# One scaling per attention step, value sums on GpSimd, and a new table of output products

## The chip, the cores and the metric

The kernel runs on one core of a Trainium2 chip. The metric is the device time of one launch in microseconds (us); lower is better. The kernel before took 1141.24 us in the median of three runs (1140.78 to 1141.5).

A core has five engines with one instruction queue each: TensorE (PE in the profile; PEld is its weight load), VectorE (DVE), ScalarE (ACT), GpSimd (POOL) and SyncE (SP), which here only issues transfers. An engine takes its instructions in order. It waits at an instruction for semaphores that other engines raise, and everything behind that instruction waits too. Matmuls write to PSUM, of which the kernel allots eight tiles of 128x512 f32; the rest of the data lies in SBUF.

## The reference

A decoder of two layers over 512 tokens of width 1024, all in f32: layer 0 mixes positions in chunks with a gated MLP; then one shared set of keys and values is computed; layer 1 is sliding-window attention over them. Each layer also has a gated MLP and a gated embedding. The change lies in layer 1's attention:

```
q = (xn @ w_q).reshape(B, nb, BLOCK, N_KV_HEADS, GQA_GROUP, HEAD_DIM)
scores = einsum('bnikgd,bnjkd->bnkgij', q, kblk) * HEAD_DIM ** -0.5
scores = where(valid, scores - slopes * dist, -inf)       # a band of 128 keys
m = maximum(max(scores, -1), sink)
e = exp(scores - m)
probs = e / (sum(e, -1) + exp(sink - m))
out = einsum('bnkgij,bnjkd->bnikgd', probs, vblk)
h = h + out.reshape(B, S, N_Q_HEADS * HEAD_DIM) @ w_o
```

There are 16 query heads of 64 channels in 4 groups (a group shares a key and value head), and 4 blocks of 128 tokens.

## The kernel before

**Numbers as pairs.** TensorE multiplies in a reduced f32 format, so every operand is split in a high part (a copy in that format) and a low part (the rest). A product is three matmuls: high by high, high by low, low by high (`mm3`, lines 181 to 183 of its inner loop). "Products" below counts matmuls of 128x128 by 128x512. Weights come in pieces of 1 MB by SyncE's transfers into `wraw`; `pump` splits each in two units, on ScalarE (`wh`, line 154) and VectorE (`wl`, line 155).

**Attention in steps.** A step is one group of heads and one block of tokens: 16 steps, `steps[i]`. The loop runs i from 0 to 17 and handles three steps at once:

- `scores(i)`: eight score matmuls into two PSUM tiles (`sc`, lines 781 and 782). VectorE picks the keys of the band from the own and the previous block (`copy_predicated`, line 784) and adds the slope with a reduction to the row's extremum (line 788). ScalarE takes four exponentials with their sums (line 793). GpSimd puts the sinks in place (line 774). The result lies in one of two halves of `prs`.
- `weights(i)`: reciprocals of the sums (line 801), then each of the four heads' weights times its reciprocal, one on VectorE (line 807) and three on ScalarE (line 805).
- `turn(i - 1)`: four transposes to PSUM (`tr`, line 822), split in `pts` (ScalarE line 252, VectorE line 253); for blocks after the first, GpSimd also cuts the part for the previous block out of both (line 830).
- `mix(i - 2)`: two or four matmuls with the values (`pv`, line 844). One half of the result's partitions holds the products with the high part of the values, the other those with the low part. They are summed: ScalarE copies the one half to `side` (line 848) and VectorE adds the other from PSUM (line 852, two instructions). Then ScalarE makes `oh` (line 856) and GpSimd `ol` (line 857), the pair that the output projection takes.

`side` is double-buffered by the parity of the step, and its copy's half was always the same partitions.

**Work beside the steps.** TensorE would stand still while the other engines do this, so the table `beside` names projection products to be issued with each step: first the values and the queries of the next groups (`project`), then the output projection (`merge(m, k0, k1)`: accumulator `o{m}`, contraction blocks k0 to k1, three matmuls each). `merge` opens its accumulator's PSUM tile at k0 = 0 and keeps it until it is complete. In steps 10 to 17 the table has 9, 9, 9, 9, 12, 6, 18 and 18 products. `more` splits one more unit of weights ahead of its use. What remains of the output projection follows the loop, where each accumulator is added to `h`.

**The order.** The order of instructions on each engine isn't written out: a scheduler takes it from the program's order, from its own idea of durations, and from priorities (`scores`, `turn` and `weights` are high). So an edit of one helper can move instructions of others. In the changed program's order of TensorE, the first pv matmul of step k is followed by transposes of step k + 1 mixed with scores of step k + 3, then the rest of pv, then the products. An exception is step 12: its first pv matmul stands right behind the last of step 11.

**Transfers of queries.** Groups 1 to 3 need their queries on other partitions, so four transfers per half group on SyncE's queue move them (lines 661 and 662), beside the loads of weights.

Of the kernel before, what the change touches and what calls it, by code (L numbers as in the profile page):

```python
# [8 lines left out]
F32 = mybir.dt.float32  # L9
F32R = mybir.dt.float32r  # L10
AF = mybir.ActivationFunctionType
ALU = mybir.AluOpType

P = 128
D = 1024
S = 512
# [10 lines left out]
GQ = HEADS // GROUPS  # L27
# [21 lines left out]
def tile_yoco(ctx: ExitStack, tc: tile.TileContext, t, out: bass.AP, out_b: bass.AP):  # L49
    nc = tc.nc  # L50
# [10 lines left out]
    def psum(name):  # L61
        return mmp.tile([P, S], F32, tag="mm", name=name)


    pieces, paired = [], set()

    def plan(ap_, n, cols, own=None):

        if own and len(own) > 1:
            m = n // len(own)  # L70
            cuts = [(q * m, m) for q in range(len(own))]
        else:
            m = n if n <= UNIT else (n // cols + 1) // 2 * cols
            cuts = [(0, m), (m, n - m)] if m < n else [(0, n)]
        pieces.append((ap_, n, cuts, own))

    def plan_cols(w, n_chunks, kk, cols=256, k0=0):
        for c in range(n_chunks):
            plan(w[c, :, k0 * cols : (k0 + kk) * cols], kk * cols, cols)
# [6 lines left out]
    def plan_ffn(l):  # L86
        for i, (j0, j1) in enumerate(PARTS):
            if i == 0:
                plan_cols(t["w_up"][l], j1, KD)
            else:  # L90
                plan_cols(t["w_up"][l, j0 + 1 : j1], j1 - j0 - 1, KD)
            if i + 1 < len(PARTS):
                plan_cols(t["w_up"][l, j1 : j1 + 1], 1, KD)
            else:
                plan(t["pT"][l], 2 * S, S, own=[(mp, "m4", "m5")])
                plan_cols(t["w_pin"][l], 2, 4)
            plan_cols(t["w_down"][l], 4, j1 - j0, k0=j0)
# [9 lines left out]
    plan_cols(t["w_q"][0:1], 1, KD)  # L107
    plan_cols(t["w_kv"][1:2], 1, KD)
    plan_cols(t["w_q"][1:4], 3, KD)
    plan_cols(t["w_o"], 4, KD)  # L110
    plan_ffn(1)
    free = [j % SLOTS for j in range(NJ, NJ + 8)]
# [4 lines left out]

    units = [(i, q, lo, n) for i, p in enumerate(pieces) for q, (lo, n) in enumerate(p[2])]
    raws, ready = {}, {}
    state = {"raw": 0, "unit": 0, "next": 0, "tags": [0, 1, 2], "turn": 0, "pt": 0}  # L120

    def load(upto, queue=nc.sync):
        while state["raw"] < min(upto, len(pieces)):
            j = state["raw"]
            a, m = pieces[j][:2]
            tags = state["tags"]
            r = wp.tile([P, 2 * UNIT], F32, tag=f"r{tags[state['turn'] % len(tags)]}", bufs=1, name=f"wraw{j}")
            state["turn"] += 1
            queue.dma_start(r[:, :m].rearrange("p (c m) -> p c m", c=2) if j in paired else r[:, :m], a)
            raws[j] = r  # L130
            state["raw"] += 1

# [70 lines left out]
    h = [hp.tile([P, S], F32, tag=f"h{k}", name=f"h{k}") for k in range(KD)]  # L203
    nc.sync.dma_start(vec[:, :KD], t["vec"][:, :KD])
    load(1, nc.scalar)
    for c in range(2):
        nc.sync.dma_start(h[0][:, c * N : (c + 1) * N], t["xT"][0][:, c * N : (c + 1) * N])
    load(2)
    nc.sync.dma_start(h[1], t["xT"][1])
    load(3)  # L210
# [18 lines left out]
    ps = psum("idle").rearrange("p (a b) -> p a b", a=4)  # L229
# [331 lines left out]
    for c in range(4):  # L561
# [4 lines left out]
        for j in range(2):  # L566
            m = 2 * c + j
            ps = ups[j]
# [13 lines left out]
            hi = ap.tile([P, S], F32R, tag=f"ah{m}", name=f"ush{m}")  # L582
# [10 lines left out]
    ps = psum("turned")  # L593
# [18 lines left out]
    sides = [slice(0, HD), slice(HD, P)]  # L612
# [28 lines left out]
    def queries(ps, g, j):  # L641


        qf = tp.tile([P, S], F32, tag="sq", name=f"qf{g}_{j}")
        m = 2 * g + j
        nc.vector.scalar_tensor_tensor(qf, ps, qscale[:, m : m + 1], rstd, op0=ALU.mult, op1=ALU.mult)
        res = [tp.tile([P, S], F32R, tag=("hs", "sg", "c0", "c1")[2 * j + e], name=f"q{g}_{j}_{e}")
               for e in range(2)]
        if g == 0:
            for e, q in enumerate(res):  # L650
                me, it = sides[e], sides[1 - e]
                nc.scalar.copy(q[me, :], qf[me, :])
                nc.vector.tensor_sub(q[it, :], qf[me, :], q[me, :].bitcast(F32))
            return res

        hi = tp.tile([P, S], F32, tag="acc", name=f"qhi{g}_{j}")
        nc.scalar.copy(hi.bitcast(F32R), qf)
        nc.vector.tensor_sub(qf.bitcast(F32R), qf, hi)
        for e, q in enumerate(res):
            me, it = sides[e], sides[1 - e]  # L660
            nc.sync.dma_start(q[me, :].bitcast(F32), hi[me, :])
            nc.sync.dma_start(q[it, :].bitcast(F32), qf[me, :])
        return res

    qs = {0: []}
    for j in range(2):
        qs[0] += queries(qps[j], 0, j)
# [42 lines left out]
    def project(g, j, k0, k1):  # L710
        if j == 0 and k0 == 0:
            box["q"] = chunk(256, KD, ahead=2)
            qs[g] = []
        if k0 == 0:
            box["qp"] = psum(f"q{g}_{j}")
        mm3(box["qp"], box["q"][k0:k1], xq[k0:k1], j * P, first=k0 == 0, last=k1 == KD)
        if k1 == KD:
            qs[g] += queries(box["qp"], g, j)
# [10 lines left out]
    def more():  # L729
# [12 lines left out]
        7: [(project, 3, 0, 4, 8), (more,)],  # L742
        8: [(project, 3, 1, 0, 4)],
        9: [(project, 3, 1, 4, 8)],
        10: [(merge, 0, 0, 3), (more,)],
        11: [(merge, 0, 3, 4), (merge, 1, 0, 2), (more,)],
        12: [(merge, 1, 2, 4), (merge, 2, 0, 1)],
        13: [(merge, 2, 1, 4)],
        14: [(merge, 0, 4, 6), (merge, 1, 4, 6)],
        15: [(merge, 2, 4, 6)],  # L750
        16: [(merge, 3, 0, 6)],
        17: [(merge, 4, 0, 6)],
    }

    def fill(i):
# [41 lines left out]
    def weights(i):  # L797

        pr, sm = live[i]
        ds = at.tile([P, GQ], F32, tag="ds", bufs=2, name=f"ds{i}")  # L800
        nc.vector.reciprocal(ds, sm)
        for e in range(GQ):
            a, r = pr[:, e, :P], ds[:, e : e + 1]
            if e:
                nc.scalar.activation(a, a, AF.Copy, scale=r)
            else:
                nc.vector.tensor_scalar_mul(a, a, r)
        live[i] = pr

    def pair(name):  # L810
# [24 lines left out]
    def mix(i):  # L835
        g, n = steps[i]
        pts = live.pop(i)
        ps = psum(f"pv{i}")
        todo = []
        for b, halves in enumerate(pts):  # L840
            both_halves = (diffs[g][:, n - 1] if b else vt[:, n, g]).rearrange("p a d -> p (a d)")
            todo += [(both_halves, x) for x in halves]
        for j, (lhs, rhs) in enumerate(todo):
            nc.tensor.matmul(ps, lhs, rhs, start=j == 0, stop=j == len(todo) - 1)


        low = side[sides[0], i % 2 * S : (i % 2 + 1) * S]
        nc.scalar.copy(low, ps[sides[1], :])
        o = side[:, 2 * S + i % 2 * N : 2 * S + (i % 2 + 1) * N].rearrange("p (b t) -> p b t", b=2)
        a, low = (x.rearrange("p (b e t) -> p e b t", b=2, e=2) for x in (ps[sides[0], :], low))  # L850
        for e in range(2):
            nc.vector.tensor_add(o[sides[e]], a[:, e], low[:, e])
        cols = slice(n * P, (n + 1) * P)
        for b in range(2):
            oh, ol = o2[2 * g + b]
            nc.scalar.copy(oh[:, cols], o[:, b, :])
            (nc.vector if i == last - 1 else nc.gpsimd).tensor_sub(ol[:, cols], o[:, b, :], oh[:, cols].bitcast(F32))

    last = len(steps)
    side = at.tile([P, 4 * S], F32, tag="vtl", name="side")  # L860
# [3 lines left out]
    for i in range(last + 2):  # L864
        if i < last:
            with tc.high_priority():
                scores(i)
        if i <= last:
            fill(i)
        if i >= 2:  # L870
            mix(i - 2)
        if i > last:
            fill(i)
        if 0 <= i - 1 < last:
            with tc.high_priority():
                turn(i - 1)
        if i < last:
            with tc.high_priority():
                weights(i)
# [46 lines left out]
    for i in range(2):  # L926
# [4 lines left out]
        for q in range(2):  # L931
            ps = psum(f"ht{i}_{q}")
# [4 lines left out]
    for m in range(4):  # L937
        ps = psum(f"gate{4 + m}")[:, :N]
# [32 lines left out]
    def gate_t(i, n):  # L971

        c0, w = cuts[i][n]
        ps = psum(f"gt{i}_{n}")[:, :w]
        end = i == 1 and n == len(cuts[i]) - 1
        if end:
            nc.tensor.matmul(ps, rows[:, :P], rows[:, P : 3 * P], start=True, stop=False)
        mm3t(ps, xs, parts2 if c0 >= S else parts, c0 % S, w, 2 + i, first=not end)
        return ps
# [57 lines left out]
    ps = gate_t(0, 1)  # L1037
# [72 lines left out]
```

## Time and profile before

| what | before |
|---|---|
| median of three runs | 1141.24 us |
| profiled execution, whole | 1141.22 us |
| its span on the core | 1139.5 us |
| TensorE busy | 1127.0 us (99%) |
| VectorE busy | 749.6 us (66%) |
| ScalarE busy | 530.0 us (47%) |
| GpSimd busy | 107.7 us (9%) |
| mean granted TensorE clock | 0.998 |
| attention's steps lie in | about 600 to 690 us |

The profile was taken in an execution of its own, which agrees with the median. Its span leaves out 1.72 us around the program. In the rows, `a<-b` is output and input by the program's names, Lnnn a line of the kernel before, `x3` a count, and a bracket or a second column names the idle time of the engine just before and what ended it. Starts are microseconds from the start of the span.

### The profile page before, as it was taken

The numbers are of one execution on the slowest core, as the hardware profiler recorded it, in microseconds if no ns is written. First come the engines' busy times: TensorE is split into PE (matmuls) and PEld (weight loads), VectorE is DVE, ScalarE is ACT, GpSimd is POOL, SyncE is SP. The second block draws the span as 40 slices with busy tenths as digits, with TensorE's granted clock in tenths as the row PEclk, the third lists the DMA queues.
The fourth block names the chain that finished last, engine by engine and source line by source line (L and its number), as shares of the span: only waits on it lengthen the run. The fifth ranks groups of instructions, "written<-read, shape, count | busy, mean of one in ns | idle before, by whom it ended". The sixth has DMA issues, their size and how long they took to land.

```text
span 1139.5 us, 13604 instructions
## 1 busy us (share of the span) xinstructions
PE 1127.0 (99%) x5266; PEld 940.5 (83%) x5266; DVE 749.6 (66%) x1158; ACT 530.0 (47%) x875; POOL 107.7 (9%) x175
## 2 busy tenths in 40 slices
PE   9999999999999999999999999999999999999997
PEld 7888888888888888888898878888888888888896
DVE  7366477763677367557988977777636763675675
ACT  6533344441344234445657985444313432355562
POOL 2000200000000000021213343000000000000222
PEclk9999999999999999999999999999999999999999
DMA  8422323223223322432224315223223233224302
GB/s 298 145 83 74 111 75 111 101 85 111 78 98 102 111 76 86 134 107 79 74 75 129 93 38 185 98 88 111 78 107 110 66 102 111 93 80 160 111 1 75
DMA packets 25776, 115.41 MB, mean 101 GB/s; under 512 B 2920, under 2 KB 8176, under 8 KB 16240
## 3 DMA queue, kind: packets, MB, share of 16 engines
q1 hardware_dynamic: 25152, 113.89, 29.8%
q8 instruction: 41, 0.67, 0.2%
q10 hardware_dynamic: 560, 0.66, 0.2%
q14 instruction: 23, 0.19, 0.1%
HBM read 108.24 MB, written 2.11 MB: 97 GB/s over the span
## 4 chain that ended last, share of the span: by engine, by line
PE 95%; DVE 2%; issue 1%; ACT 1%; DMA 1%; POOL 0%; SPq 0%; POOLq 0%; DVEq 0%; ACTq 0%
PE up L181 14%; PE up L183 14%; PE up L182 14%; PE d L183 8%; PE d L181 8%; PE d L182 8%; PE gate L181 2%; PE gate L183 2%; PE gate L182 2%; PE u L182 1%; PE u L183 1%; PE u L181 1%; PE o L182 1%; PE o L181 1%; PE o L183 1%; PE q L181 1%
## 5 line engine op out<-in xcount | busy, mean ns | idle before, releaser
L154 ACT CAST wh<-wraw 128x1024 fp32r<-128x1024 f32 (+2 forms) x197 | 202.0, 1028 | 264.6 <-PE d L182 131.0
L155 DVE TENSOR_TENSOR wl<-wraw,wh 128x1024 fp32r<-128x1024 f32 (+1 forms) x198 | 238.4, 1205 | 127.9 <-ACT wh L154 127.6
L181 PE MATMUL up<-nf00h,wh 128*128 128x512 f32 x352 | 137.1, 390 | 0.0
L181 PE MATMUL up<-nf10h,wh 128*128 128x512 f32 x352 | 137.0, 389 | 0.0
L182 PE MATMUL up<-nf00l,wh 128*128 128x512 f32 x352 | 136.9, 389 | 0.0
L183 PE MATMUL up<-nf00h,wl 128*128 128x512 f32 x352 | 136.9, 389 | 0.0
L183 PE MATMUL up<-nf10h,wl 128*128 128x512 f32 x352 | 136.9, 389 | 0.0
L182 PE MATMUL up<-nf10l,wh 128*128 128x512 f32 x352 | 136.9, 389 | 0.0
L181 PE MATMUL d<-ah,wh 128*128 128x512 f32 x352 | 136.9, 389 | 0.0
L182 PE MATMUL d<-al,wh 128*128 128x512 f32 x352 | 136.9, 389 | 0.0
L183 PE MATMUL d<-ah,wl 128*128 128x512 f32 x352 | 136.9, 389 | 0.0
L379 ACT ACTIVATE c<-hs,vec 128x512 f32<-128x512 f32 x88 | 71.5, 815 | 72.0 <-DVE hs L375 71.2
L380 DVE SCALAR_TENSOR_TENSOR c<-hs,vec,c 128x511 f32<-128x511 f32 x88 | 65.8, 749 | 34.5 <-ACT c L379 34.4
L355 DVE TENSOR_TENSOR h<-h,d 128x512 f32<-128x512 f32 x56 | 38.4, 686 | 73.8 <-PE d L183 73.8
L252 ACT CAST ah<-a 128x512 fp32r<-128x512 f32 x44 | 27.4, 622 | 109.5 <-DVE a L385 109.4
L183 PEld LDWEIGHTS up<-nf10h,wl 128*128 128x128 f32 x352 | 66.1, 188 | 13.8
L182 PEld LDWEIGHTS d<-al,wh 128*128 128x128 f32 x352 | 66.1, 188 | 13.8
L183 PEld LDWEIGHTS up<-nf00h,wl 128*128 128x128 f32 x352 | 66.1, 188 | 13.8
L183 PEld LDWEIGHTS d<-ah,wl 128*128 128x128 f32 x352 | 66.1, 188 | 13.7
L182 PEld LDWEIGHTS up<-nf00l,wh 128*128 128x128 f32 x352 | 66.1, 188 | 13.7
L182 PEld LDWEIGHTS up<-nf10l,wh 128*128 128x128 f32 x352 | 66.1, 188 | 13.7
L181 PEld LDWEIGHTS d<-ah,wh 128*128 128x128 f32 x352 | 66.1, 188 | 13.6
(454 smaller groups left out, 2061.7 us busy)
## 6 DMA issues: line engine op xcount, KB each, us to landing
wraw<-in_w_up SPq DMA_DIRECT2D x44, 1024.0 KB, 4.8
wraw<-in_w_down SPq DMA_DIRECT2D x16, 896.0 KB, 4.6
wraw<-in_w_down SPq DMA_DIRECT2D x8, 1024.0 KB, 4.8
wraw<-in_w_gate SPq DMA_DIRECT2D x8, 1024.0 KB, 4.8
wraw<-in_w_u SPq DMA_DIRECT2D x4, 1024.0 KB, 5.9
wraw<-in_w_out SPq DMA_DIRECT2D x4, 1024.0 KB, 4.8
wraw<-in_w_q SPq DMA_DIRECT2D x4, 1024.0 KB, 4.9
wraw<-in_w_o SPq DMA_DIRECT2D x4, 1024.0 KB, 4.9
```

Of the source, the lines that this page charges most:

```text
L154: nc.scalar.copy(hi, src)
L155: nc.vector.tensor_sub(low, src, hi.bitcast(F32))
L181: nc.tensor.matmul(ps, wh[:, a:b], xh, start=st, stop=False)
L182: nc.tensor.matmul(ps, wh[:, a:b], xl, start=False, stop=False)
L183: nc.tensor.matmul(ps, wl[:, a:b], xh, start=False, stop=en)
L252: nc.scalar.copy(hi, src)
L355: nc.vector.tensor_add(h[m], h[m], ps)
L379: nc.scalar.activation(c, hs, AF.Identity, bias=v("conv_b", l * 2 * NJ + col), scale=cw[2])
L380: nc.vector.scalar_tensor_tensor(c[:, 1:], hs[:, : S - 1], cw[1], c[:, 1:], op0=ALU.mult, op1=ALU.add)
```

## The change

The four scalings of a step become one VectorE multiply over 128 x 4 x 128 with the reciprocals broadcast along the keys. In `mix` ScalarE copies both halves of pv to `side`, at partitions that alternate with the step, and GpSimd does the two sums, from SBUF to SBUF. The table has 12 products in each of steps 10 to 15 (24 of them stand together for steps 14 and 15, all needing the third group's `oh` and `ol`), then 18 and 18; the accumulators o0 to o3 are open by step 13 (before: o0 to o2), and o5 comes into step 17. The 18 products more in the table come from behind the loop. One more `more` stands at step 12. `behind` orders the second and third load of w_o after the transfers of the second and third group's second half.

```diff
+    outs = len(pieces)
     plan_cols(t["w_o"], 4, KD)
...
+    def behind(ins, front):
+
+        tc.add_manual_dep(ins.ins, front.ins.name,
+                          mybir.DependencyInfo(mybir.DependencyClass.NoSync, mybir.DependencyReason.DATA),
+                          reason="order")
...
-            queue.dma_start(r[:, :m].rearrange("p (c m) -> p c m", c=2) if j in paired else r[:, :m], a)
+            ins = queue.dma_start(r[:, :m].rearrange("p (c m) -> p c m", c=2) if j in paired else r[:, :m], a)
+            for front in state["sent"].pop(j, []):
+                behind(ins, front)
...
-            nc.sync.dma_start(q[me, :].bitcast(F32), hi[me, :])
-            nc.sync.dma_start(q[it, :].bitcast(F32), qf[me, :])
+            sent = [nc.sync.dma_start(q[me, :].bitcast(F32), hi[me, :]),
+                    nc.sync.dma_start(q[it, :].bitcast(F32), qf[me, :])]
+            if g > 1 and j:
+                state["sent"].setdefault(outs + g - 1, []).extend(sent)
...
-        10: [(merge, 0, 0, 3), (more,)],
-        11: [(merge, 0, 3, 4), (merge, 1, 0, 2), (more,)],
-        12: [(merge, 1, 2, 4), (merge, 2, 0, 1)],
-        13: [(merge, 2, 1, 4)],
+        10: [(merge, 0, 0, 2), (merge, 1, 0, 2), (more,)],
+        11: [(merge, 0, 2, 4), (merge, 1, 2, 4), (more,)],
+        12: [(merge, 2, 0, 4), (more,)],
+        13: [(merge, 3, 0, 4)],
         14: [(merge, 0, 4, 6), (merge, 1, 4, 6)],
-        15: [(merge, 2, 4, 6)],
-        16: [(merge, 3, 0, 6)],
-        17: [(merge, 4, 0, 6)],
+        15: [(merge, 2, 4, 6), (merge, 3, 4, 6)],
+        16: [(merge, 4, 0, 6)],
+        17: [(merge, 5, 0, 6)],
...
-        for e in range(GQ):
-            a, r = pr[:, e, :P], ds[:, e : e + 1]
-            if e:
-                nc.scalar.activation(a, a, AF.Copy, scale=r)
-            else:
-                nc.vector.tensor_scalar_mul(a, a, r)
+        a = pr[:, :, :P]
+        nc.vector.tensor_mul(a, a, ds.rearrange("p (e o) -> p e o", o=1).to_broadcast([P, GQ, P]))
...
-        low = side[sides[0], i % 2 * S : (i % 2 + 1) * S]
-        nc.scalar.copy(low, ps[sides[1], :])
         o = side[:, 2 * S + i % 2 * N : 2 * S + (i % 2 + 1) * N].rearrange("p (b t) -> p b t", b=2)
-        a, low = (x.rearrange("p (b e t) -> p e b t", b=2, e=2) for x in (ps[sides[0], :], low))
+        two = [side[sides[i % 2], x * S : (x + 1) * S] for x in range(2)]
+        for x in range(2):
+            nc.scalar.copy(two[x], ps[sides[x], :])
+        a, low = (x.rearrange("p (b e t) -> p e b t", b=2, e=2) for x in two)
         for e in range(2):
-            nc.vector.tensor_add(o[sides[e]], a[:, e], low[:, e])
+            nc.gpsimd.tensor_add(o[sides[e]], a[:, e], low[:, e])
```

More of the change, by code (lines that the diff above doesn't have):

```diff
@@ L119, in tile_yoco @@
     raws, ready = {}, {}
-    state = {"raw": 0, "unit": 0, "next": 0, "tags": [0, 1, 2], "turn": 0, "pt": 0}
+    state = {"raw": 0, "unit": 0, "next": 0, "tags": [0, 1, 2], "turn": 0, "pt": 0, "sent": {}}
+    def behind(ins, front):
+        tc.add_manual_dep(ins.ins, front.ins.name,
+                          mybir.DependencyInfo(mybir.DependencyClass.NoSync, mybir.DependencyReason.DATA),
+                          reason="order")
     def load(upto, queue=nc.sync):
```

## The prediction

> **What bounds the kernel now.** I read the page first: the busy times and the chain that ended last.
>
> ```profile
> span 1139.5 us, 13604 instructions
> PE 1127.0 (99%) x5266; PEld 940.5 (83%) x5266; DVE 749.6 (66%) x1158; ACT 530.0 (47%) x875; POOL 107.7 (9%) x175
> PE 95%; DVE 2%; issue 1%; ACT 1%; DMA 1%; POOL 0%; SPq 0%; POOLq 0%; DVEq 0%; ACTq 0%
> ```
>
> TensorE is the bound everywhere, so a change that leaves its matmuls alone can only move the moments at which it stands still. The second view is the busy time by stretches of 10 us around attention (columns: PE, PEld, DVE, ACT, POOL, each with its count, then clock, DMA share, GB/s).
>
> ```profile
> 630.00:640.00 10.00, 10.00 (x57) 8.57 (x56) 9.88 (x36) 9.90 (x37) 3.80 (x9) 1.00 0.52 161
> 640.00:650.00 10.00, 9.89 (x55) 8.17 (x54) 8.83 (x32) 9.30 (x29) 4.84 (x10) 1.00 0.24 52
> 650.00:660.00 10.00, 8.37 (x49) 6.62 (x50) 9.51 (x40) 9.79 (x37) 3.27 (x8) 1.00 0.25 54
> 660.00:670.00 10.00, 8.78 (x45) 6.76 (x44) 7.80 (x26) 8.85 (x31) 5.45 (x12) 1.00 0.30 106
> 670.00:680.00 10.00, 9.31 (x45) 7.33 (x46) 8.01 (x29) 7.92 (x30) 5.16 (x8) 1.00 0.01 2
> 680.00:690.00 10.00, 9.98 (x45) 7.75 (x44) 4.40 (x9) 4.31 (x10) 3.03 (x6) 1.00 0.52 191
> ```
>
> TensorE is full until 640, with ScalarE and VectorE at 9.9 of 10, and then has holes until 680. From 612 to 648 each step carries twelve projection products; the holes start with the steps that carry nine output products. Who is waited for, from the waits of 600 to 690:
>
> ```profile
> PE tr L822 <- DVE prs L807: 1.7, 3, 0.8
> PE o L182 <- POOL ol L857: 0.7, 1, 0.7
> PE tr L822 <- DVE pts L253: 0.5, 1, 0.5
> PE pv L844 <- ACT prs L793: 0.4, 1, 0.4
> PE o L181 <- ACT oh L856: 0.3, 1, 0.3
> ```
>
> Busy time counts the tail of a pipelined matmul, so a hole's price is read from start to start in the timeline:
>
> ```profile
> 649.27 0.39 PE L183 MATMUL o<-oh,wl 128*128 128x512 f32 x1
> 649.50 0.39 PE L844 MATMUL pv<-pts,vt 128*128 128x512 f32 x1
> 650.68 0.41 PE L822 MATMUL tr<-ident,prs 128*128 128x128 f32 x2 [0.80 <-DVE prs L807]
> 660.90 0.49 PE L181 MATMUL o<-oh,wh 128*128 128x512 f32 x1
> 662.11 0.50 PE L182 MATMUL o<-ol,wh 128*128 128x512 f32 x1 [0.71 <-POOL ol L857]
> ```
>
> A product takes 0.23 of the queue (649.27 to 649.50). So the first hole costs 1.18 - 0.23 = 0.95 and the other 1.21 - 0.23 = 0.98: 0.15 to 0.27 above the bracketed idle time. The waits above sum to 3.6 in 7 holes; with some 0.2 for each they cost 5.0. Small delays behind them (products 0.3 apart, pieces under 0.5 at the last two steps) I take at 1.2 more. So 6.2 us is the most that the change can win: 1141.2 - 6.2 = 1135.0.
>
> **The change part by part.** Durations (mean ns after busy time), from groups in the same stretch, the GpSimd sum from the output norm:
>
> ```profile
> L852 DVE TENSOR_TENSOR side<-pv,side 64x256 f32<-64x256 f32 x32 | 13.3, 416 | 3.8 <-ACT side L848 3.4
> L807 DVE TENSOR_SCALAR prs<-prs,ds 128x128 f32<-128x128 f32 x15 | 6.3, 417 | 0.2
> L658 DVE TENSOR_TENSOR qf<-qf,qhi 128x512 fp32r<-128x512 f32 x6 | 4.1, 684 | 0.2 <-ACT qhi L657 0.2
> L793 ACT ACTIVATE prs<-prs,neg 128x129 f32<-128x129 f32 x56 | 22.1, 397 | 3.2 <-DVE neg L788 2.4 <-POOL ol L857 0.6
> L805 ACT ACTIVATE prs<-prs,ds 128x128 f32<-128x128 f32 x45 | 14.9, 395 | 0.0
> L154 ACT CAST wh<-wraw 128x1024 fp32r<-128x1024 f32 x9 | 9.4, 1043 | 0.7 <-PE o L182 0.5 <-DMA wraw<-in_w_q 0.2
> L657 ACT CAST qhi<-qf 128x512 fp32r<-128x512 f32 x6 | 3.7, 618 | 2.2 <-DVE qf L646 2.2
> L848 ACT COPY side<-pv 64x512 f32<-64x512 f32 x16 | 9.3, 583 | 2.9 <-PE pv L844 2.4
> L856 ACT CAST oh<-side 128x128 fp32r<-128x128 f32 x32 | 8.0, 294 | 3.0 <-DVE side L852 2.8
> L857 POOL TENSOR_TENSOR ol<-side,oh 128x128 fp32r<-128x128 f32 x30 | 14.1, 490 | 4.3 <-ACT oh L856 4.2
> L912 POOL TENSOR_TENSOR facc<-facc,fsq x6: 737/741/1021, 1104.7 to 1113.4; 128x256 f32<-128x256 f32 x6
> ```
>
> 1. Scaling. ScalarE loses three scalings, VectorE swaps one of 0.42 for a multiply over 128x512. The nearest row is L658, also 128x512 from two SBUF inputs: 0.68. All four heads now wait for one instruction, instead of ScalarE's three. ScalarE's queue timing:
>
> ```profile
> 641.46 0.58 ACT L848 COPY side<-pv 64x512 f32<-64x512 f32 x1
> 641.95 0.99 ACT L805 ACTIVATE prs<-prs,ds 128x128 f32<-128x128 f32 x3
> 642.84 1.04 ACT L154 CAST wh<-wraw 128x1024 fp32r<-128x1024 f32 x1
> ```
>
> The three hold the queue for 0.89, a copy for 0.49.
>
> 2. Value sums. ScalarE gains a copy (+0.49), so it nets -0.4 per step. VectorE loses two sums of 0.42. GpSimd gains two; it has no 64x256 row, and L912 at the same 256 elements per lane gives 0.74 each. The bounds are VectorE's own 0.42 below and L912's 1.02 above; I take 0.74, the same engine and length. So GpSimd gains 1.5 a step. The way from the end of pv to ol grows from 0.58 + 0.83 + 0.29 + 0.49 = 2.2 to 1.07 + 1.5 + 0.29 + 0.49 = 3.35, handoffs aside: +1.15. Behind the wait stands ScalarE: oh is in its queue ahead of the next exponentials and pts copies, with two exponentials between copies and oh. Behind GpSimd's sums stand the next step's selects, nsink copies and ol.
>
> The Trainium skill (GPSIMD Engine Reference, section 3.1) puts an add at 4497 ns on GpSimd against 2293 on VectorE. By that ratio of 1.96 the pair would take, as an estimate, 1.6 us, where L912 gives 1.5.
>
> 3. The twelve products. Steps 10 to 13 carry 12 instead of 9, 9, 9, 9, fed from products that stood after the loop; TensorE's work is unchanged. A step of 12 is 12 x 0.23 + pv, transposes and scores 2.3 = 5.06 us. ScalarE's work per step: four exponentials of 0.40 (1.6), pts 0.49 (taken as the copy), two copies 1.07, two oh 0.4 (each starts before the one ahead has ended), and for casts of weights and queries 9.4 + 3.7 = 13.1 over 90 us, 0.7 a step: 4.3 in all. Its wait for the sums is their 1.5 less the two exponentials of 0.8, so 0.7. That is 5.0 against 5.06: it just fits. Counted from a step's first pv: copies end at 3.5, sums at 5.1, oh at 5.5, the last exponential at 6.3, the multiply at 7.2, and the transposes that need it start two steps on, at 10.3. So the multiply has 3 us to spare, and the first four holes, at 649.5, 654.0, 657.6 and 660.9 (three behind the scaling, 1.7 + 0.6, and 0.98 behind ol: 3.3 us) go. What would be late next is below.
>
> 4. The banks. o3 is opened at step 13, so o0 to o3, the pv of step 11, tr and two score tiles fill the eight PSUM tiles of the pool. In the changed order of TensorE, pv of step 12 therefore waits for both copies of step 11's pv, and no product stands between them. Copies at 0.49 + 0.58 plus two handoffs of about 0.13 give at least 1.3. With the cast of w_o and a pts copy ahead of them in ScalarE's queue and step 10's oh late by GpSimd's sums, I estimate 2.0.
>
> 5. The 24 products of steps 14 and 15 now follow at once, and need oh and ol of step 11. On GpSimd these are queued sums, select, ol, select, ol; on ScalarE after four exponentials and a pts copy. From the transposes of step 13: pts 0.5, two exponentials 0.8, oh 0.3, ol 0.46 make 2.2 with handoffs, against 1.3 of TensorE's own work (a pv matmul and eight of scores): 0.9; the second ol comes behind a select of 0.63, so 0.4 more. Together with item 4: 2.7 at least (1.3 + 0.9 + 0.4, rounded up), 3.6 with everything between (2.0 + 0.9 + 0.4, and 0.3 for the first ol), 4.7 if the split of a weight on VectorE (as long as its cast, 1.04) also holds step 12's pts.
>
> 6. Tail. pv of step 15 stands without products between transposes and itself: 0.7, where the steps now lose 0.5. The last oh waits for step 14's sums on GpSimd: 0.85 before o0's last products, where now nothing is lost.
>
> 7. The loads. The second and third load of w_o stand behind the queries' transfers in SP's queue before and after alike, so the ordering costs nothing. Where this cover is wrong, a late w_o stops ScalarE's cast; the page has 4.9 us from issue to landing, and my margin is about 1 us.
>
> ```profile
> wraw<-in_w_o SPq DMA_DIRECT2D x4, 1024.0 KB, 4.9
> ```
>
> Sum: removed 6.2; new 3.6 + 0.7 + 0.85 = 5.15. That is -1.05 on the profiled execution's 1141.22 (span 1139.5 and 1.72 around it), which equals the median of 1141.24. So 1140.2. By the bounds of item 5 it is 1139.3 to 1141.3.
>
> **GpSimd beside VectorE.** One price isn't in the sum. These rows stand together in the timeline:
>
> ```profile
> 640.49 0.68 DVE L658 TENSOR_TENSOR qf<-qf,qhi 128x512 fp32r<-128x512 f32 x1
> 640.53 1.14 POOL L830 TENSOR_SCALAR_AFFINE_SELECT pts<-p6l 128x512 fp32r<-128x512 f32 x1
> 641.68 0.29 DVE L807 TENSOR_SCALAR prs<-prs,ds 128x128 f32<-128x128 f32 x1
> 649.58 0.87 POOL L857 TENSOR_TENSOR ol<-side,oh 128x128 fp32r<-128x128 f32 x2
> 649.95 0.58 DVE L807 TENSOR_SCALAR prs<-prs,ds 128x128 f32<-128x128 f32 x1
> 673.37 0.63 POOL L830 TENSOR_SCALAR_AFFINE_SELECT pts<-p13l 128x512 fp32r<-128x512 f32 x1
> ```
>
> A select of 0.63 took 1.14 beside a two-input VectorE subtraction; a scaling of 0.29 took 0.58 beside GpSimd. The slowed one loses 0.3 to 0.5. After the change GpSimd works about 4 of 5.06 us per step, and the multiply has two inputs.
>
> The Trainium skill (SBUF — State Buffer, section "Who interferes with whom") calls this an exclusive lock: a VectorE instruction with two SBUF inputs and a GpSimd one that reads SBUF block each other for the whole instruction. The trace agrees (0.63 to 1.14), and the page speaks against the change.
>
> **The rivals.**
>
> *Faster than 0.2%.* The oh and ol chains run ahead, since ScalarE is 0.4 a step lighter, and only the inescapable parts of items 4 to 6 remain, partly covered: 1.3 + 0.9 + 0.7 + 0.3 = 3.2 lost. Gain 3.0: 1138.2. For it: no hole at 612 to 648, with both engines at 9.9. Against: the order puts nothing between pv of steps 11 and 12.
>
> *Slower.* GpSimd's sums set the pace of ScalarE. If each step's select or sum loses 0.5 beside VectorE, sums end 0.5 later, oh waits 1.2, and ScalarE needs 5.5 per step. Over steps 4 to 11 that is 8 x 0.45 = 3.6, less some slack of 1, and items 4 and 5 rise by 1 with everything late: -1.05 + 3.6 = +2.6, 1143.8. It decides once ScalarE's step passes 5.06. For it: the 1.14 row, and 4.2 us that POOL already waits for oh. Against: only 0.5 to 1 such meeting per step is likely, often hidden behind a weight cast.
>
> *Nothing happens in the loop.* The multiply, blocked by GpSimd (0.68 + 0.6), replaces L807 as what the transposes wait for, so half of the 3.3 stays: 1140.2 + 1.6 = 1141.8, also within 0.2%.
>
> **How the numbers follow.** 0.2%, about what a measurement of this kernel can tell from no change, is 2.3 us: 1138.9 to 1143.5. Forecast 0.30, blocked multiply 0.13, faster rival 0.29, slower rival 0.25, a late load or something not seen 0.03 (1143 to 1146). Thus faster 0.29, same 0.43, slower 0.28. The forecast's own range is 1139.0 to 1142; with both rivals, 1137.0 to 1144.8, a tenth left out on each side.
>
> **What would show it.** Right: no hole of transposes behind the scaling between 649 and 661; a hole of 1.3 to 2.0 where pv of step 12 waits for ScalarE's side copy; one behind GpSimd's ol at the first of the 24 products; a wait of nearly 1 for oh after the last pv; sums of about 0.74; ScalarE waiting 0.7 per step for GpSimd's side. Wrong: sums far from 0.74, transposes still behind the multiply, holes already in steps 4 to 9 (then the slower rival), or no hole at pv of step 12 (then the faster). A hole behind a weight cast that waits for its load would be item 7.

## The result and the profile after

The changed kernel takes 1157.63 us in the median of four runs (1156.61 to 1158.77), against 1141.21 us before. The ratio is 1.0144, with a 95% interval of 1.0127 to 1.0162. That is 16.4 us slower. The profiled execution took 1158.77 us with a span of 1157.1, so 17.6 us lie between the two profiled spans; that difference is taken apart below.

The busy times of the changed kernel, and its stretches of 10 us in attention:

```profile
span 1157.1 us, 13569 instructions
PE 1133.7 (98%) x5266; PEld 943.5 (82%) x5266; DVE 745.3 (64%) x1126; ACT 526.0 (45%) x843; POOL 135.9 (12%) x207
```

```profile
620.00:630.00 10.00, 10.00 (x57) 8.60 (x56) 6.62 (x22) 7.74 (x25) 7.07 (x12) 1.00 0.18 40
630.00:640.00 10.00, 7.96 (x45) 6.18 (x45) 7.37 (x24) 7.39 (x21) 5.18 (x9) 1.00 0.53 160
640.00:650.00 10.00, 9.24 (x45) 7.10 (x44) 6.58 (x23) 7.35 (x25) 5.92 (x11) 1.00 0.24 53
650.00:660.00 10.00, 7.68 (x42) 6.07 (x42) 7.92 (x28) 8.12 (x24) 6.09 (x11) 1.00 0.12 26
660.00:670.00 10.00, 8.00 (x33) 6.42 (x34) 5.90 (x19) 6.73 (x22) 7.25 (x12) 0.83 0.42 133
670.00:680.00 10.00, 9.34 (x52) 7.53 (x51) 6.26 (x23) 6.53 (x23) 6.01 (x10) 1.00 0.00 1
680.00:690.00 10.00, 6.27 (x26) 4.90 (x25) 7.75 (x26) 7.87 (x23) 6.69 (x11) 0.83 0.29 106
```

ScalarE and VectorE are less busy than before (7.4 of 10 at 630 to 640, against 9.9), and TensorE has holes there that it didn't have. So no engine is full: they wait for each other. The waits from 600 to 710 say where, first those of ScalarE, then those of TensorE (600 to 740):

```profile
ACT oh L864 <- POOL side L860: 19.7, 15, 1.9
ACT prs L804 <- DVE neg L799: 5.4, 10, 0.8
```

```profile
PE pv L851 <- ACT pts L261: 3.6, 3, 1.6
PE o L190 <- ACT oh L864: 3.2, 2, 2.3
PE pv L851 <- ACT side L857: 3.0, 1, 3.0
PE nf1ms L311 <- DVE nf1quarter L303: 1.3, 1, 1.3
PE o L191 <- POOL ol L865: 0.7, 1, 0.7
```

ScalarE stands at `oh` for GpSimd's sums in 15 of 16 steps, 1.3 us in the mean. Behind `oh` in its queue are two exponentials and the copies of transposed weights (`pts`), for which TensorE then waits. The wait of transposes behind the scaling (before: 1.7 us) is gone. Two steps in the timeline, on GpSimd, ScalarE, VectorE and TensorE (other instructions left out):

```profile
633.63 2.67 POOL L860 TENSOR_TENSOR side<-side 64x256 f32<-64x256 f32 x2 [3.17 <-ACT side L857]
634.47 1.23 DVE L164 TENSOR_TENSOR wl<-wraw,wh 128x1024 fp32r<-128x1024 f32 x1
636.30 0.39 PE L192 MATMUL q<-n11h,wl 128*128 128x512 f32 x1
636.33 0.50 ACT L864 CAST oh<-side 128x128 fp32r<-128x128 f32 x2 [1.94 <-POOL side L860]
637.64 0.58 ACT L261 CAST pts<-tr 128x512 fp32r<-128x512 f32 x1
638.28 0.50 PE L851 MATMUL pv<-pts,vt 128*128 128x512 f32 x1 [1.59 <-ACT pts L261]
639.61 0.63 POOL L837 TENSOR_SCALAR_AFFINE_SELECT pts<-pts 128x512 fp32r<-128x512 f32 x1 [0.57 <-PE tr L829]
640.21 1.54 POOL L860 TENSOR_TENSOR side<-side 64x256 f32<-64x256 f32 x2
641.79 0.50 ACT L864 CAST oh<-side 128x128 fp32r<-128x128 f32 x2 [1.07 <-POOL side L860]
```

The `oh` that starts late at 636.33 makes the `pts` copy late, and TensorE stands from its last product at 636.30 to the pv matmul at 638.28.

A pair of sums takes 1.54 alone. Beside the split of a weight on VectorE it takes 2.67, 1.1 more, about the split's 1.23; two of the 15 waits at `oh` stand behind such a pair (1.9 each). The pair at 640.21 is alone, but stands behind a select in GpSimd's queue. The Trainium skill (SBUF — State Buffer, "Who interferes with whom") says that such a pair of instructions excludes each other for a whole instruction; the 2.67 agrees with that.

Then a cost that no part of the prediction had. The first hole of TensorE of over 2 us, and what follows it:

```profile
659.25 0.40 PE L851 MATMUL pv<-pts,vt 128*128 128x512 f32 x1
661.96 0.50 PE L190 MATMUL o<-oh,wh 128*128 128x512 f32 x1 [2.31 <-ACT oh L864]
...
663.80 0.63 PE L192 MATMUL o<-oh,wl 128*128 128x512 f32 x1
664.23 0.63 PE L190 MATMUL o<-oh,wh 128*128 128x512 f32 x1
664.66 0.63 PE L191 MATMUL o<-ol,wh 128*128 128x512 f32 x1
```

A product now takes 0.43 from start to start instead of 0.23, for about 3 us. The granted clock by stretch:

```profile
662.00:667.00 5.00, 4.96 (x14) 3.66 (x15) 3.30 (x13) 3.42 (x12) 3.83 (x7) 0.66 0.60 213
667.00:677.00 10.00, 10.00 (x57) 8.39 (x55) 6.05 (x21) 7.32 (x23) 6.10 (x13) 1.00 0.00 0
683.00:688.00 5.00, 4.64 (x18) 3.80 (x18) 3.82 (x16) 3.93 (x16) 3.41 (x6) 0.66 0.57 211
734.00:739.00 5.00, 4.96 (x16) 3.97 (x17) 2.17 (x8) 0.33 (x1) 1.02 (x1) 0.66 0.27 111
```

It falls three times between 600 and 740: behind the holes of 2.7 us (above) and 3.4 us (679.9 to 683.3), both from start to start, and behind the holes at the norm, below. Each time that costs up to (1 - 0.66) x 5.0 = 1.7 us, less what a hole behind it hides: 5.1 at most. Before, with holes of at most 1.2 us, the clock stayed at 1.00 throughout attention. The size of a single hole doesn't settle it: behind the 2.0 us before 638.28 the clock stayed at 1.00 too:

```profile
639.00:643.00 4.00, 4.00 (x24) 3.45 (x24) 2.64 (x11) 2.41 (x12) 2.94 (x6) 1.00 0.21 84
```

The Trainium skill (TensorE: Matmul & The Clock Gate, Part 1) gives 426.7 ns for a cold matmul over 512 columns and some 3.4 us of work until the clock is back; the trace agrees with 0.43 from start to start and about 3 us.

The last new hole lies behind the loop, at the norm's first matmul:

```profile
732.31 0.39 PE L192 MATMUL up<-nf10h,wl 128*128 128x512 f32 x1
734.04 0.39 PE L311 MATMUL nf1ms<-nf1quarter,alike 128*128 128x16 f32 x2 [1.34 <-DVE nf1quarter L303]
```

The sum over the profiled spans, by landmarks. The last pv matmul starts at 701.9 instead of 685.8: 16.1 later. Ahead of it stand 91 output products instead of 75, 16 x 0.23 = 3.7; the other 12.4 are further holes and slow clock. From there to the norm's first matmul it is 32.1 us instead of 32.3, though 16 products fewer stand in that stretch. Behind that 1.7 are added, as much as the slow clock there costs. So 16.1 - 0.2 + 1.7 = 17.6.

### The profile page after: what moved, and what is told of

Read it like the earlier page. It is cut to its first block, busy times and chain, and to the rows that moved or that the text cites. A ratio compares the mean times of both kernels' runs of the same rounds, so it can differ in the third digit from the quotient of the medians.

```text
span 1157.1 us, 13569 instructions
## 1 busy us (share of the span) xinstructions
PE 1133.7 (98%) x5266; PEld 943.5 (82%) x5266; DVE 745.3 (64%) x1126; ACT 526.0 (45%) x843; POOL 135.9 (12%) x207
## 5 line engine op out<-in xcount | busy, mean ns | idle before, releaser
L190 PEld LDWEIGHTS up<-nf10h,wh 128*128 128x128 f32 x352 | 66.5, 189 | 13.8
```

Source lines behind the costliest of these rows:

```text
L190: nc.tensor.matmul(ps, wh[:, a:b], xh, start=st, stop=False)
```

## The experiments

Times are medians; "before" is the kernel before on the same chip. Letters: G for the sums on GpSimd (with the two copies), M for the multiply, T for the table.

### One part alone

G alone:

```diff
-        low = side[sides[0], i % 2 * S : (i % 2 + 1) * S]
-        nc.scalar.copy(low, ps[sides[1], :])
...
+        two = [side[sides[i % 2], x * S : (x + 1) * S] for x in range(2)]
+        for x in range(2):
+            nc.scalar.copy(two[x], ps[sides[x], :])
...
-            nc.vector.tensor_add(o[sides[e]], a[:, e], low[:, e])
+            nc.gpsimd.tensor_add(o[sides[e]], a[:, e], low[:, e])
```

> The kernel before with one part of the change: two ScalarE copies and two GpSimd sums in mix; scaling and table as before. Theory P (pace): ScalarE stands in its queue at oh for GpSimd's sums, about 1.3 us in each step, and that sets the pace of the steps. Then this kernel is 8 to 14 us slower than before (1149 to 1155), with TensorE holes already in steps 4 to 9, behind ScalarE's pts copies, and no hole behind the loop's end (o5 is not in the loop). Rival B (banks and table: o0 to o3 open, 24 products together): without the new table the sums cost little, within 3 us of before. Rival M (the multiply over four heads, blocked by GpSimd): little, within 3 us, since the multiply is not here.

Measured: 1154.73 us, before 1141.12 (ratio 1.0112, 1.0095 to 1.0129). The pace theory's range: +13.6, with TensorE waiting from step 4 on. But ScalarE's wait at `oh` is 10.0 us in 12 waits, 0.8 each and not 1.3, and TensorE waits for GpSimd's selects (3.1) about as long as for ScalarE's copies of transposed weights (3.0, and 1.0 at step 4). ScalarE keeps its three scalings here and is busy 9.1 of 10 from 640 to 650. So the time agrees with the theory and the mechanism in part. This part alone is most of the loss.

M alone:

```diff
-        for e in range(GQ):
-            a, r = pr[:, e, :P], ds[:, e : e + 1]
...
+        a = pr[:, :, :P]
+        nc.vector.tensor_mul(a, a, ds.rearrange("p (e o) -> p e o", o=1).to_broadcast([P, GQ, P]))
```

> The kernel before with only the scaling changed: one VectorE multiply over four heads in place of one VectorE and three ScalarE scalings. Theory: the three holes behind L807 at 649 to 659 come from a ScalarE queue that is full (9.8 of 10); 0.89 us a step less there takes them away, and 1 to 3 us are won: 1138 to 1140.3. Rival M: the multiply is blocked by GpSimd or simply longer (0.75 against 0.42) and the transposes wait for it: 1141 to 1145.

Measured: 1144.40 us, before 1141.13 (1.0033, 1.002 to 1.0046). The rival's range. Busy time from 650 to 670 of this run:

```profile
650.00:660.00 10.00, 8.22 (x48) 6.60 (x47) 9.87 (x41) 8.40 (x31) 5.51 (x12) 1.00 0.25 54
660.00:670.00 10.00, 8.78 (x49) 7.05 (x47) 8.68 (x23) 6.57 (x21) 4.45 (x9) 1.00 0.31 106
670.00:680.00 10.00, 7.78 (x25) 5.55 (x25) 7.48 (x29) 6.04 (x23) 2.88 (x4) 0.55 0.00 0
```

ScalarE is lighter (8.4 instead of 9.8), VectorE is full (9.87 instead of 9.51), and the transposes wait for it as before. The holes from 668 on grew and brought the slow clock (0.55). This profiled execution took 1146.42 us at a mean clock of 0.994, the median one 1144.40 at 0.997, so not all of that slow stretch is part of the 3.3 us. The rows read as two full engines, of which the change relieved one and loaded the other; no run tests that by itself.

T alone (the expectation names the order of the loads too; the kernel that ran has only the table):

```diff
-        10: [(merge, 0, 0, 3), (more,)],
+        10: [(merge, 0, 0, 2), (merge, 1, 0, 2), (more,)],
...
-        17: [(merge, 4, 0, 6)],
+        17: [(merge, 5, 0, 6)],
```

> The kernel before with only the new table (and the order of the two loads, which changes no instruction's place). Theory: twelve products a step hide the chains of steps 8 to 12, but o5 in the loop bares the norm behind it (3.9 us with the slow clock): 1140 to 1144. Rival B: four open accumulators and 24 products together cost holes of 2 us and more at steps 12 to 14: above 1146.

Measured: 1147.60 us, before 1141.13 (1.0054, 1.0038 to 1.007), in rival B's range. B's mechanism doesn't show: the profiled execution (1146.55 us) has no hole of 2 us in attention, 1.5 from start to start is the largest, and the one at pv of step 12 is 1.2. In that execution (span 1144.8) the last pv starts at 691.0, 5.2 later than before: 3.7 for the 16 products, and 1.5 us more of holes, not less. Twelve products don't hide the steps' chains; the holes only lie elsewhere. The three parts alone lose 13.6 + 3.3 + 6.5 = 23.4, more than the 16.4 of the whole, so their losses overlap. From 650 to 660, with ScalarE and VectorE at 9.2 and 9.4:

```profile
650.00:660.00 10.00, 7.99 (x45) 6.24 (x44) 9.39 (x41) 9.21 (x35) 3.77 (x8) 1.00 0.54 157
```

### One part taken away

Without G (mix as before):

> The changed kernel with mix as before (one ScalarE copy, VectorE sums from PSUM); multiply and new table stay. Theory P: the holes of steps 4 to 13 behind ScalarE go; what remains is at most the hole at the norm behind the loop (3.9 us with the slower clock after it): 1139 to 1145. Rival B: holes of 2 to 3 us at pv of step 12 and at the 24 products stay: above 1148. Rival M: above 1148, with transposes waiting for the multiply.

Measured: 1143.62 us, before 1141.12 (1.0025, 1.0015 to 1.0035), in the pace theory's range. The holes of steps 4 to 7 are gone, and at pv of step 12 and at the 24 products TensorE waits 0.6 us at most. Its profiled execution (1146.16 us, 2.5 above the median) still has two holes of 1.65 and 1.1 us from start to start at step 11's products, which wait for `oh` and `ol`, with slow clock behind them; the 3.7 of products moved ahead; and the hole at the norm.

Without T (table as before):

> The changed kernel with the table as before; multiply and GpSimd sums stay. The table alone put 16 more products (3.65 us) ahead of the last pv and had as many holes as before. If these products only push the last pv back, the time is 5 us below the changed kernel's, 1152 to 1154. If in the changed kernel they stand in holes that ScalarE and GpSimd make anyway, it stays within 2 us of it: 1156 to 1159.

Measured: 1154.81 us, before 1141.45 (1.0117, 1.0099 to 1.0135). Neither range: 2.8 below the changed kernel. The last pv comes at 697.9 instead of 701.9, 4.0 earlier, which is about what 16 products take (3.7). So beside G they fill no holes either. From there to the norm it is then 33.7 us instead of 32.1, and that takes 1.6 back.

Without M (scaling as before):

> The changed kernel with the scaling as before (one on VectorE, three on ScalarE); sums and table stay. If ScalarE is what holds the steps once it waits for GpSimd, 0.89 us a step more in its queue makes this slower than the changed kernel: 1160 to 1166. If the multiply costs what it cost alone on VectorE (3.3 us), it is faster: 1153 to 1156.

Measured: 1157.57 us, before 1141.45 (1.0141, 1.0124 to 1.0157), the changed kernel's own time. Neither expectation held: beside G and T it doesn't matter where the scaling stands.

Without o5's products in step 17:

```diff
-        17: [(merge, 5, 0, 6)],
```

> The changed kernel with the 18 products of o5 taken out of step 17 and back behind the loop. Theory C (lost cover): the holes behind the loop (2.1 us around the norm's first matmul and 1.7 us of slow clock behind them) come from too little TensorE work after the loop, which is 18 x 0.23 = 4.1 us shorter. Then this kernel is 3 to 4 us faster than the changed one, 1153.5 to 1155, and TensorE's idle time at the norm is under 0.3 us. If the norm is late for another reason (GpSimd's sums of squares behind attention's), it stays within 1 us of 1157.6.

Measured: 1157.03 us, before 1141.12 (1.014, 1.0125 to 1.0155). Theory C failed in its consequence. The hole at the norm is gone (TensorE waits under 0.3 there), but a hole of 2.4 us stands at o0's last products, which wait for the last `oh` (1.0 in the changed kernel). The time lost only changed its place. The time is in the other expectation's range, yet the norm isn't late here as that one had it. In both kernels 91 output products start ahead of the last pv: o5's stand behind it either way, and the edit only changes their place among those that follow.

Without G and without o5 in step 17, both edits together:

> Multiply and new table with mix as before, and o5's products back behind the loop. The run without the GpSimd sums kept 3.9 us at the norm behind the loop. If that is lost cover, it goes here, less what then shows at the last oh and ol (about 0.5 with VectorE's sums; the GpSimd version lost 2.4 there): 1139 to 1141.5, so at least as fast as before. If the norm is late for another reason: 1143 to 1145.

Measured: 1142.69 us, before 1141.13 (1.0013, 1.0004 to 1.0023), between the two ranges. The hole at the norm stayed at 1.5 us. So it isn't simply lost cover. VectorE is what nearly fills the stretch from the first residual addition to the norm's matmul, here in the kernel before, the changed one, and the one with T alone:

```profile
691.12:718.13 27.01, 27.01 (x121) 22.34 (x119) 22.75 (x25) 15.54 (x22) 9.11 (x6) 1.00 0.38 131
```

```profile
709.36:734.04 24.68, 22.90 (x100) 18.32 (x99) 22.84 (x25) 14.39 (x21) 9.37 (x6) 1.00 0.32 106
```

```profile
696.74:721.80 25.06, 23.36 (x102) 18.70 (x100) 22.75 (x24) 14.51 (x21) 9.80 (x6) 1.00 0.34 113
```

VectorE is busy for 22.8 us there in all three. Before, TensorE has 27 us of matmuls beside it; in the others 23, and holes. That VectorE sets the norm is read from these rows; no run gives it less to do there. With the new table, 16 fewer products follow the last pv, 3.7 us of work, but the way from it to the norm is only 1.5 us shorter (30.8 with T alone, 32.3 before) or 1.6 (32.1 in the changed kernel, 33.7 without T). So a product moved ahead of the last pv delays what follows by its whole length and saves less than half of it behind.

### What of the sums costs: the engine, or ScalarE's standing still

Sums on VectorE, after the same two copies:

```diff
-            nc.gpsimd.tensor_add(o[sides[e]], a[:, e], low[:, e])
+            nc.vector.tensor_add(o[sides[e]], a[:, e], low[:, e])
```

> The changed kernel with the two sums of a step on VectorE instead of GpSimd, still from SBUF, after two ScalarE copies; all else as changed. If GpSimd's duration (1.54 a pair, 2.67 beside a weight split) is what ScalarE waits for, the wait at oh falls from 1.3 to about 0.5 a step, the holes of steps 4 to 9 go, and the time is 1142 to 1148. If it is the second copy and the in-order queue of ScalarE whatever engine sums, it stays above 1151.

Measured: 1149.17 us, before 1141.12 (1.007, 1.0055 to 1.0085), 8.5 below the changed kernel. It lies 1.2 above the range for GpSimd's duration and well below the other. ScalarE's wait at `oh` fell further than expected, from 19.7 to 3.1 us. The run without G also has its sums on VectorE, so the 5.5 us between the two are the price of the second copy and of the sums that wait for it. Of the 14.0 us between the changed kernel and the one without G, then, 8.5 go with the engine of the sums and 5.5 with the second copy.

Sums on GpSimd, and `oh` on GpSimd too:

```diff
-            nc.scalar.copy(oh[:, cols], o[:, b, :])
+            nc.gpsimd.tensor_copy(oh[:, cols], o[:, b, :])
```

> The changed kernel with oh also made by GpSimd, in the same queue as the sums and ol, so that ScalarE waits for no GpSimd result between its side copies and its next exponentials; GpSimd gets two casts of about 0.45 a step more. If the cost lies in ScalarE standing still in its order (19.7 us in 15 waits), the holes of steps 4 to 9 behind pts copies go: 1143 to 1150. If the length of the way from pv to ol, or GpSimd's own load (then some 5 us a step), sets the pace, it stays at 1153 or above, with TensorE waiting for ol and for selects.

Measured: 1148.67 us, before 1141.13 (1.0064, 1.0049 to 1.0079), in the first range. GpSimd does more work than in the changed kernel, its sums take as long, and still 9 us are won. The sums in the changed kernel, and GpSimd's two groups in this run:

```profile
L860 POOL TENSOR_TENSOR side<-side 64x256 f32<-64x256 f32 x32 | 25.7, 805 | 13.4 <-ACT side L857 12.3
...
L860 POOL TENSOR_TENSOR side<-side 64x256 f32<-64x256 f32 x32 | 25.8, 805 | 5.1 <-ACT side L857 3.7
L864 POOL CAST oh<-side 128x128 fp32r<-128x128 f32 x32 | 14.4, 478 | 1.0
```

ScalarE's standing for GpSimd falls from 19.7 to 5.1 us. So GpSimd's load doesn't make the large loss, and the sums' duration makes it only through who waits for them. This run also takes the casts' work from ScalarE, so a last run keeps every instruction on its engine and only moves the wait. In it `oh` stands behind all four exponentials:

```diff
-            nc.scalar.copy(oh[:, cols], o[:, b, :])
+            cast = nc.scalar.copy(oh[:, cols], o[:, b, :])
+            if i + 3 in exps:
+                behind(cast, exps[i + 3])
```

(with `oh` and `ol` of step i - 3 written after `scores(i)`, and `exps[i]` the last exponential of step i.)

> The changed kernel with the same instructions on each engine; only ScalarE's order is tied so that oh of a step stands behind all four exponentials of the third step after it, instead of behind two. If the cost is ScalarE standing at oh (1.3 us a step), 0.8 us of that wait is filled with the two exponentials and the steps get some 0.5 to 0.8 shorter while ScalarE paces them: 1147 to 1152. If it is the work that the change adds to the engines, or the length of the way from pv to ol, nothing is won: 1156 to 1160.

Measured: 1153.03 us, before 1141.49 (1.0106, 1.0091 to 1.0121), 4.6 below the changed kernel, 1 above the range. ScalarE's wait fell from 19.7 to 13.0, and TensorE's for the `pts` copies behind it from 3.6 to 1.2:

```profile
ACT oh L871 <- POOL side L860: 13.0, 11, 2.0
PE pv L851 <- ACT pts L261: 1.2, 2, 0.7
```

6.7 us less of standing brought 4.6. Up to 1.7 of that is the clock, which falls twice here up to 740 (0.57 from 677 to 681, and again from 728 to 732) and not three times. The wait is a cause by itself, since no work changed its engine. How the difference of 4.4 between this run and the one before it divides between the waits that stay and ScalarE's casts isn't shown.

### Attempts at a better kernel

The kernel before with `oh` on GpSimd, with the first scaling on GpSimd, and with the later `oh` (its own edits only, as above; for the second):

```diff
-                nc.vector.tensor_scalar_mul(a, a, r)
+                nc.gpsimd.tensor_scalar_mul(a, a, r)
```

> The kernel before with one edit of its own: oh by GpSimd instead of ScalarE, sums on VectorE as before. ScalarE loses 0.4 us a step and its waits for the sums; GpSimd, busy 3 to 5 of 10, gains 0.9. If the holes before come from a ScalarE that is full, they shrink by 1 to 3 us: 1138 to 1140. If VectorE is what is full there, or if ol comes too late behind oh on GpSimd, 1141 to 1145.

Measured: 1143.15 us, before 1141.45 (1.0015, 1.0006 to 1.0025): slower, in the second range; the transposes wait for VectorE's scaling 2.5 us instead of 1.7.

> The kernel before with one edit of its own: the first head's scaling on GpSimd instead of VectorE (line 807). VectorE loses 0.28 to 0.58 a step, ScalarE nothing. If the holes behind that scaling are a full VectorE's, they shrink: 1138.5 to 1140.5. If ScalarE's exponentials set them, or GpSimd's scaling comes behind its selects and ol, 1141 to 1146.

Measured: 1141.72 us, before 1141.45 (1.0003, 0.9993 to 1.0012): no difference. The transposes now wait 2.6 us for GpSimd's scaling.

> The kernel before with the same tie: oh behind all four exponentials of the third step after it. There ScalarE waits only 2.8 us in all for VectorE's sums, so at most about 1 us is won (1140 to 1141.3); if ol then comes too late for the products of steps 14 and 15 or for the last ones, up to 1143.

Measured: 1141.32 us, before 1141.49 (0.9999, 0.999 to 1.0009): no difference. No run beat the kernel before.

## Why the prediction was wrong, point by point

- **The bound.** The reading that TensorE sets the end and only its holes can move held. The limit of the gain, 6.2 us, wasn't tested, since nothing was gained.
- **Scaling (1).** The multiply measured 0.75 against 0.68 taken. No transposes waited for it in the changed kernel, as forecast. But alone it made the kernel 3.3 us slower. The step that took ScalarE's relief as a gain left out that VectorE, at 9.5 to 9.9 of 10 in two of the rows quoted, was full too; that this is the cause is read from the rows.
- **Value sums (2).** The duration was right: 0.81 in the mean, against 0.74. The failed step is the sentence that ScalarE's wait is the sums' 1.5 less two exponentials, 0.7 a step. It measured 1.3 in the mean of 15 waits, 19.7 us in all. Four of them were 0.7 to 0.9, as forecast. The others show what the sentence left out: four of 1.05 to 1.3 behind selects ahead of the sums in GpSimd's queue; two of 1.9 where a weight's split on VectorE stretched the pair to 2.67; and five of 1.1 to 1.9 in which fewer than two exponentials stood between the copies and `oh`, above all in the last three steps, which have none left. Only the second of these was in the text, as a price that "isn't in the sum". And the second copy, which the sum of ScalarE's work counted as covered, goes with 5.5 us.
- **The balance (3).** 4.3 + 0.7 = 5.0 against 5.06 "just fits" was the decision, and it hung on 0.06 us. With 1.3 it is 5.6. The holes come from step 4 on, as the slower rival said they would. Its wait at `oh`, 1.2, was near the mark; its reason, 0.5 lost beside VectorE in every step, shows in two of the waits only. Its price of 3.6 us was too small by far. It had no price for the products moved ahead of the last pv (3.7), for the clock (up to 5.1 in three places), or for the hole at step 11's products (659.25 to 661.96).
- **Twelve products hide the chains (3).** Wrong, as T alone shows: 1.5 us more of holes ahead of the last pv than before. That 612 to 648 had no hole was read as cover; a lead that the steps still had there explains it as well, and no run tells when it is spent.
- **The banks (4).** Place and mechanism right, size not: 1.3 to 2.0 forecast, 3.2 measured (679.9 to 683.3), behind ScalarE's side copies, which were late.
- **The 24 products (5).** Place right: a hole of 0.9 behind the first `ol`, against 0.9 + 0.4.
- **The tail (6).** 0.7 measured 0.6; the last `oh` 0.85 measured 1.0. Right.
- **Behind the loop.** The prediction priced nothing there. It took products moved into the loop to save behind it what they cost in it. But the way to the norm got only 0.2 us shorter for 3.7 us of products fewer: 2.1 us of holes stand at the norm, and up to 1.7 of slow clock follow. That is the term it missed; that VectorE's 22.8 us set it is a reading.
- **The loads (7).** TensorE waits for no load of w_o here, as forecast; the ordering wasn't run by itself, and T alone leaves it out.

## What to carry to other kernels

When work goes to an idle engine, ask first which engine waits for its result in its own queue, and what stands behind that wait; the same slow sums were 9 us cheaper here once ScalarE, freed of the cast too, no longer stood at them. A balance that fits by 1% of a step isn't a balance: put the queues ahead of the waited-for instruction and the collisions between engines into the sum, and ask in which steps the work that shall cover a wait is there at all. And work that is moved into a loop to fill holes delays everything behind the loop unless the holes are really filled and the stretch behind gets shorter by as much, so look at which engine paces the stretch that follows.

## What was unexpected of the hardware

Holes are given from start to start here. In the kernel before, holes of TensorE up to 1.2 us left the clock at 1.00. In the changed kernel those of 2.7 and 3.4 us, and the pair of 0.8 and 1.7 at the norm, were each followed by some 3.4 us at half speed (0.43 instead of 0.23 for a product over 512 columns), up to 1.7 us lost each. But the length of a hole gives no rule. With the later `oh`, one of 2.9 us left the clock at 1.00:

```profile
654.91 0.39 PE L851 MATMUL pv<-pts,vt 128*128 128x512 f32 x1
657.82 0.50 PE L190 MATMUL o<-oh,wh 128*128 128x512 f32 x1 [2.52 <-ACT oh L871]
...
658.00:661.00 3.00, 2.82 (x12) 2.05 (x13) 2.51 (x11) 2.86 (x9) 2.88 (x7) 1.00 0.83 333
```

With M alone, holes of at most 1.25 us between 666 and 671, where TensorE was busy 3.4 of 5 us, were followed by half speed from 671 to 681:

```profile
671.00:681.00 10.00, 8.20 (x26) 5.92 (x25) 7.35 (x28) 5.89 (x23) 3.66 (x6) 0.50 0.00 0
```

What decides isn't shown by these runs. So a long hole can cost up to 1.7 us more than its length, and need not.
